# Half of q as a seventeenth pair of seven products, with new places and engines for the last tiles' block sums

## The chip, the cores and the metric

The kernel runs on one core of a Trainium2 chip. The metric is the device time of one execution in microseconds. A core has a matrix engine (TensorE, PE in the profile; PEld is its weight load), three engines for elementwise work (VectorE = DVE, ScalarE = ACT, GpSimd = POOL) and SyncE (SP), which here issues the DMA transfers. Each engine works through its own instructions strictly in order; engines wait for each other by semaphores. Matrix products accumulate in PSUM, which has 8 banks of 128 x 512 float32; GpSimd does not read PSUM in this kernel.

## The reference

One layer of an encoder over a sequence of 1024 positions (a 16 x 64 grid) with 1024 channels, in float32:

```python
h = layer_norm(x, emb_ln_g, emb_ln_b)
proj = h @ w_in                                   # 1024 x 5120
q, k, v, z_a, u, z_b, g_a, g_b = jnp.split(proj, offs, axis=-1)
attn = neighbourhood_attention(q, k, v, rpb)      # 8 heads x 64, window 8 x 16, q scaled by 1/8
y_a = attn * silu(z_a)
u = centred_depthwise_conv(u, conv_w, conv_b)
hr = rg_lru(u, ..., False) + rg_lru(u, ..., True) # gated linear recurrence, both directions
y_b = hr * silu(z_b)
m = sigmoid(g_a + b_merge[0]) * (y_a @ w_ba) + sigmoid(g_b + b_merge[1]) * (y_b @ w_bb)
return layer_norm(ALPHA * h + m @ w_out, ln_g, ln_b)
```

q, k, v, z_a, u and z_b have 512 columns each, g_a and g_b 1024 each. The change concerns the 512 columns of q, which are four blocks (m = 0 to 3) of 128.

## The kernel before

**Precision.** A float32 operand is split into a high part (rounded to fp32r) and a low part (the rest, `lo_of`). A product of two operands is three matrix products, high x high, low x high, high x low (`mm3`).

**Stage 1: normalize, turn, v and half of q.** The sequence is eight tiles of 128 positions. Each tile is normalized, transposed on PE (`turn`, two banks `tp` per tile) and stored transposed as four blocks B11, B12, B21, B22: the first index is the half of the 1024 input channels, the second the half of the sequence. ACT makes the high parts (`turn_hi`), DVE the low parts (`turn_lo`, from the bank). v is computed tile by tile (`v_part`, 24 products), q by blocks of 128 columns and halves of the sequence (`q_part(m, n)`: 8 channel blocks x 3 = 24 products of 128 x 512 in one bank). `q_hi`, `q_lo` and `q_store` scale a q result by 1/8, split it and store it (512 KB).

**Block sums.** For tiles 4 to 7 the second stage needs sums of the four blocks, T1 to T4: `t_full(i)` makes T1, T2, T3 (one ACT copy from PSUM into a place for T3, then four DVE instructions, three of which read PSUM), `t_last(i)` makes T4 (two DVE instructions, both operands in SBUF), `t_hi` casts the high parts on ACT, `t_lo` subtracts the low parts on GpSimd. The T3 copies of all four tiles have the tag "a22" with two places, of which one still holds a weight tile of v until v is done.

**Stage 2: sixteen pairs of seven products.** The other columns are computed two blocks (256 columns) at a time, in the manner of Strassen and Winograd: a pair takes seven products (`OPS`: a11, a12, s2, s1, s3, s4, a22) of 4 channel blocks x 3 = 12 matrix products, where plain multiplication takes eight. Weights of a pair are four loads of 256 KB (`s_load`), four sums (`s_sum`, DVE, operands in SBUF), seven high parts (`s_hi`) and seven low parts (`s_lo`). For pair 0 the high parts are made on ACT, before the loop; for later pairs most are made on GpSimd, one pair ahead. Seven slots of the loop make a pair: in slot k product k runs on PE, the bank of product k - 1 is emptied (`evacuate`: ACT copies u1, u2, u3, DVE additions, then what the pair's `take_...` does with the result), and work for the next pair is issued. Products accumulate into one another's banks (`INTO`: s2, s3 and a22 into the bank of a11, s4 into that of s1), so that a bank has to be read out between two of them.

**Work spread over the slots.** `at(slot, ...)` puts the convolution (`conv_stage`) and the recurrence (`gate_stage`) beside the products; CONV_AT, GATE_AT, LATE_AT and HEAD_AT are their first slots. `U_PAIRS` are the pairs whose result is u; they need no extra bank. The constants of the recurrence (sp, nsp, from `lru_lambda`) are some 30 small DVE instructions issued at once ahead of the loop (lines 626 to 642).

**Order and places.** The order of all engines is the order of the program text. PSUM banks of stage 1 come from the pool ps0 (four banks, assigned by the list `places`) and pst0 (four banks); the loop uses psd (two banks) and ps6 (six banks), which lie over the old ones, and a new tile waits only for the tile whose bank it takes. The tag "x" has five places of 4 KB per partition, used by the input tiles and then by the block sums T1, T2 and T4.

**Around the join** the order is: v of tiles 4 and 5 with `tile_in` of 6 and 7 between, v of 6 and 7 (lines 559 to 592), then `q_part` for (0,1), (1,1), (2,0), (2,1), (3,0), (3,1) with the preparation of pair 0 spread between them (lines 593 to 612), the loads of pair 1, the new pools, the rates, and the loop.

## Time and profile before

| what | us |
|---|---|
| median of 3 runs | 678.4 (678.39 to 678.75) |
| profiled execution, its own time | 678.46 |
| its span, first to last instruction | 676.7 |
| PE busy | 665.2 |
| stage 1 up to the first product of a pair | 0 to 105.4 |
| the sixteen pairs | 105.4 to 426.2 |
| attention, with the first merge products as filling | to 541.9 |
| merge and output projection | to 676.7 |

Times within the execution are counted from the start of the span. A line of a timeline gives start, duration, engine, line of the code, operation, output <- inputs, shapes, and in brackets how long the engine had been idle and what ended that. The chain of waits gives start, duration and what ran. A matrix product of 128 x 512 shows 0.39 us from its start to its end, but the next one starts before that end; the distance of starts is what counts.

### The profile page before, as it was taken

The numbers are of one execution on the slowest core, as the hardware profiler recorded it, in microseconds if no ns is written. First come the engines' busy times: TensorE is split into PE (matmuls) and PEld (weight loads), VectorE is DVE, ScalarE is ACT, GpSimd is POOL, SyncE is SP. The second block draws the span as 40 slices with busy tenths as digits, with TensorE's granted clock in tenths as the row PEclk, the third lists the DMA queues.
The fourth block names the chain that finished last, engine by engine and source line by source line (L and its number), as shares of the span: only waits on it lengthen the run. The fifth ranks groups of instructions, "written<-read, shape, count | busy, mean of one in ns | idle before, by whom it ended". The sixth has DMA issues, their size and how long they took to land.

```text
span 676.7 us, 9344 instructions
## 1 busy us (share of the span) xinstructions
PE 665.2 (98%) x3201; PEld 555.7 (82%) x3201; DVE 492.7 (73%) x821; ACT 364.5 (54%) x612; POOL 355.8 (53%) x258
## 2 busy tenths in 40 slices
PE   8999999999999999999999999999999999999995
PEld 6888888888888887888788888888888878888884
DVE  6978747886998699879967785477787787443434
ACT  6554433256786676669576634477777554210110
POOL 6798632434677576567647444116155456334442
PEclk9999999999999999999999999999999999999998
DMA  8654353233434133431553456998793467412211
GB/s 326 244 179 170 122 206 126 77 110 123 125 128 144 40 103 115 170 126 48 195 178 122 173 191 254 316 366 296 255 323 132 162 220 281 178 62 94 93 63 62
DMA packets 48702, 113.39 MB, mean 168 GB/s; under 512 B 5056, under 2 KB 9744, under 8 KB 47120
## 3 DMA queue, kind: packets, MB, share of 16 engines
q1 hardware_dynamic: 48624, 112.81, 47.2%
q8 instruction: 25, 0.41, 0.3%
q14 instruction: 21, 0.17, 0.1%
q10 hardware_dynamic: 32, 0.01, 0.0%
HBM read 77.11 MB, written 35.68 MB: 167 GB/s over the span
## 4 chain that ended last, share of the span: by engine, by line
PE 89%; DVE 6%; DMA 2%; issue 1%; SPq 1%; ACT 0%; POOL 0%; DVEq 0%; POOLq 0%
PE a L134 30%; PE o L134 13%; PE mb L134 12%; PE s L134 11%; PE q L134 6%; PE v L328 6%; PE acc L1107 3%; PE s L1061 3%; PE pt L1083 3%; PE g L759 2%; DMA wqk_s<-in_w_qk_dram 2%; DVE ws_l L128 1%; PE tp L270 1%; DMA rsb<-rs_d 1%; DVE uc L717 1%
## 5 line engine op out<-in xcount | busy, mean ns | idle before, releaser
L134 PE MATMUL o<-wo_h,ml 128*128 128x512 f32 (+1 forms) x136 | 51.2, 377 | 0.0
L134 PE MATMUL o<-wo_l,mh 128*128 128x512 f32 (+1 forms) x136 | 51.2, 376 | 0.0
L134 PE MATMUL o<-wo_h,mh 128*128 128x512 f32 (+1 forms) x136 | 51.2, 376 | 0.0
L134 PE MATMUL a<-ht_h,ws_h 128*128 128x512 f32 x128 | 50.0, 390 | 0.0
L134 PE MATMUL a<-ht_l,ws_h 128*128 128x512 f32 x128 | 49.8, 389 | 0.0
L134 PE MATMUL a<-ht_h,ws_l 128*128 128x512 f32 x128 | 49.8, 389 | 0.0
L134 PE MATMUL a<-b_h,wa_h 128*128 128x512 f32 x128 | 49.8, 389 | 0.0
L134 PE MATMUL a<-b_h,wa_l 128*128 128x512 f32 x128 | 49.8, 389 | 0.0
L134 PE MATMUL a<-b_l,wa_h 128*128 128x512 f32 x128 | 49.8, 389 | 0.0
L1071 DVE CUSTOM_DVE_ANT_0 sc<-s,bias 128x384 f32<-128x384 f32 (+1 forms) x64 | 33.4, 522 | 21.6 <-PE s L1061 14.2
L1361 DVE SCALAR_TENSOR_TENSOR z<-z,o 128x512 f32<-128x512 f32 (+1 forms) x17 | 11.2, 656 | 51.0 <-PE o L134 51.0
L1091 ACT CAST pt_h<-pt 128x384 fp32r<-128x384 f32 x64 | 29.0, 453 | 25.3 <-PE pt L1083 17.3
L1371 POOL TENSOR_TENSOR z<-z,gb 128x1024 f32<-128x1024 f32 x7 | 16.8, 2400 | 48.5 <-ACT z L1370 48.5
L1076 ACT ACTIVATE p<-sc,summ 128x384 f32<-128x384 f32 (+1 forms) x64 | 37.8, 591 | 5.5 <-DVE summ L1071 5.3
L1340 ACT ACTIVATE sd<-mv,eps_z 128x1 f32<-128x1 f32 x8 | 2.4, 294 | 67.1 <-DVE mv L1366 67.1
L128 DVE TENSOR_TENSOR pt_l<-pt,pt_h 128x384 fp32r<-128x384 f32 x64 | 33.2, 519 | 2.1 <-ACT pt_h L1091 1.6
L328 PE MATMUL v<-wv,b_h 128*128 128x512 f32 x128 | 32.9, 398 | 0.6 <-ACT b_h L279 0.5
L867 POOL CAST wb_h<-wb 128x512 fp32r<-128x512 f32 x9 | 7.0, 779 | 47.4 <-DMA wb<-in_w_bb_dram 47.4
L1061 PE MATMUL s<-ks,qs 128*128 128x384 f32 (+1 forms) x128 | 31.4, 327 | 0.0
L1083 PEld LDWEIGHTS pt<-ident,p 128*128 128x128 f32 x176 | 23.1, 140 | 8.5
L1083 PE MATMUL pt<-ident,p 128*128 128x128 f32 x176 | 29.6, 272 | 0.0
L128 POOL TENSOR_TENSOR wb_l<-wb,wb_h 128x512 fp32r<-128x512 f32 x16 | 22.0, 1375 | 14.3 <-ACT wb_h L865 13.6
(438 smaller groups left out, 2204.2 us busy)
## 6 DMA issues: line engine op xcount, KB each, us to landing
ks<-k_d SPq DMA_DIRECT2D x8, 1024.0 KB, 7.5
h_d<-x SPq DMA_DIRECT2D x8, 512.0 KB, 5.0
v_d<-vs SPq DMA_DIRECT2D x8, 512.0 KB, 3.7
q_d<-q SPq DMA_DIRECT2D x8, 512.0 KB, 3.1
ga_d<-ga SPq DMA_DIRECT2D x16, 256.0 KB, 2.2
gb_d<-gb SPq DMA_DIRECT2D x16, 256.0 KB, 2.6
k_d<-k SPq DMA_DIRECT2D x8, 512.0 KB, 3.4
qs<-q_d SPq DMA_DIRECT2D x8, 512.0 KB, 5.5
```

What stands on the lines that cost most here:

```text
L128: eng.tensor_tensor(lo, full, hi.bitcast(F32), ALU.subtract)
L134: PE.matmul(o, a, b, start=first and i == 0, stop=last and i == len(prods) - 1, skip_group_check=not (first and last))
L328: PE.matmul(vos[i][:], a, wv[kind == "w"][k][:], start=vn[i] == 0, stop=vn[i] == 23)
L759: PE.matmul(o[:, n, :], w[:, 2 * d + b, :], us[b][:, n * HALF:(n + 1) * HALF], start=z == 0, stop=z == 1)
L1061: PE.matmul(o[:, :P * len(near(t))], q[:, t * P:(t + 1) * P], k[:, z, keys], start=z == 0, stop=z == 1)
L1071: V.tensor_tensor_reduce(s[:, :w], o[:, :w], heads[h][2][:, b0:b0 + w], -1.0, 3.0e38, ALU.add, ALU.min, accum_out=sums[h][0][:, t:t + 1])
L1076: A.activation(probs[h % 2][t][:], scs.pop((h, t))[:, :w], AF.Exp, bias=sums[h][0][:, t:t + 1], scale=-1.0, accum_out=sums[h][1][:, t:t + 1])
L1083: PE.transpose(tp[:, n * P:(n + 1) * P], probs[h % 2][t][:, z * P:(z + 1) * P], ident[:])
L1091: A.copy(pt[0][:, span(b)], tps[h, b][:, :P * len(near(b))])
L1107: PE.matmul(acc[g][:, d:d + w], vvs[h // 2][:, b, h % 2, :], pt[:, a:a + w], start=b in (1, 6) and z == 0, stop=z == 1 and b == (4, 7)[g])
L1361: V.scalar_tensor_tensor(z[:, cols], z[:, cols], ALPHA * TWICE, o, ALU.mult, ALU.add)
L1371: G.tensor_tensor(z[:], z[:], gb2[:, 0, :], ALU.mult)
```

## The change

The number of pairs becomes 17. Pair 0 is now the q columns of blocks m = 2 and 3 (a new `take_q`), which `q_part` computed before; all other pairs move up by one, and with them the slots of the convolution, the recurrence and what follows (by seven). `qk_load(2)`, `qk_load(3)` and their `qk_prep` go.

Around it: the four weight blocks of pair 0 are loaded into two "x" places instead of their usual ones; its sums stand ahead of v of tile 7, its high and low parts between v of tile 7 and the two q groups that are left, (0,1) and (1,1); all its low parts are made on DVE. The T3 copies of tiles 4 to 7 get the tags a22, a21, a12, a22. `t_last` of tiles 5, 6 and 7 goes from DVE to GpSimd and moves, with `t_hi`, `t_lo` and `t_full`, to other places in the order. The rates become a generator whose six parts are issued in slots 1 to 6.

```diff
-N_PAIR = 16
+N_PAIR = 17
-CONV_AT = (7, 24, 45, 66)
-GATE_AT = (14, 24, 35, 45, 56, 66, 77, 87)
-LATE_AT = (102, 102, 103, 104, 105)
-HEAD_AT = 109
+CONV_AT = (14, 31, 52, 73)
+GATE_AT = (21, 31, 42, 52, 63, 73, 84, 94)
+LATE_AT = (109, 109, 110, 111, 112)
+HEAD_AT = 116
-U_PAIRS = (0, 5)
+U_PAIRS = (1, 6)
...
     def t_full(i):
-        tt[i, 3] = wsp.tile([P, 4, P], F32, tag="a22", bufs=2, name=f"t3_{i}")[:]
+        tag = ("a22", "a21", "a12", "a22")[i - 4]
+        tt[i, 3] = wsp.tile([P, 4, P], F32, tag=tag, bufs=2 if tag == "a22" else 1, name=f"t3_{i}")[:]
...
     def t_last(i):
-        t4 = tt[i, 4]
-        V.tensor_tensor(t4, f(B21[0], i), tt[i, 2], ALU.subtract)
-        V.tensor_tensor(t4, t4, f(B21[1], i), ALU.add)
+        t4, eng = tt[i, 4], V if i == 4 else G
+        eng.tensor_tensor(t4, f(B21[0], i), tt[i, 2], ALU.subtract)
+        eng.tensor_tensor(t4, t4, f(B21[1], i), ALU.add)
...
     def s_load(p, *names):
+        for z, o in enumerate(names if p < N_PAIR else ()):
+            if p:
+                t = wsp.tile([P, 4, P], F32, tag=o, bufs=2 if o == "a22" else 1, name=f"{o}_{p}f")[:]
+            else:
+                if z == 0:
+                    both = ln.tile([P, 2, 4, P], F32, tag="x", bufs=5, name=f"{o}_{p}f")
+                t = both[:, z]
+            SP.dma_start(t, w_s[p, ("a11", "a21", "a12", "a22").index(o)])
...
     def s_lo(p, o):
         if p < N_PAIR:
             hi, lo = s_w[p, o]
-            lo_of(G if o in LO_POOL else V, lo[:], s_a[p, o][:], hi[:])
+            lo_of(G if p and o in LO_POOL else V, lo[:], s_a[p, o], hi[:])
```

The order from `q_store(0, 0)` to the loop, after the change (before, `t_last(5)` follows `q_store(1, 0)`, and the other steps stand as described above):

```python
    keep(7)
    t_full(5)
    q_part(1, 0)
    t_last(5)
    q_hi(1, 0); q_lo(1, 0); q_store(1, 0)
    for kind in "hwa": v_part(4, kind, KS)
    tile_in(6)
    v_hi(4)
    t_hi(5, 2, 1, 3)
    tile_lo(6)
    v_lo(4); v_store(4)
    t_full(6)
    t_hi(5, 4)
    t_lo(5, 2, 1, 3, 4)
    t_last(6)
    for kind in "hwa": v_part(5, kind, KS)
    tile_in(7)
    v_hi(5)
    t_hi(6, 2, 1, 3)
    tile_lo(7)
    v_lo(5); v_store(5)
    t_full(7)
    t_hi(6, 4)
    t_lo(6, 2, 1, 3, 4)
    t_last(7)
    s_load(0, "a21", "a22"); s_load(0, "a11", "a12"); s_load(1, "a21")
    for kind in "hwa": v_part(6, kind, KS)
    v_hi(6); v_lo(6); v_store(6)
    t_hi(7, 2, 1, 3)
    s_sum(0, "s1", "s2", "s3", "s4")
    for kind in "hwa": v_part(7, kind, KS)
    s_load(1, "a12")
    v_hi(7); v_lo(7); v_store(7)
    for o in OPS[:3]: s_hi(0, o); s_lo(0, o)
    t_hi(7, 4)
    t_lo(7, 2, 1, 3, 4)
    s_load(1, "a11"); s_load(1, "a22")
    q_part(0, 1)
    for o in OPS[3:5]: s_hi(0, o); s_lo(0, o)
    q_hi(0, 1); q_lo(0, 1); q_store(0, 1)
    q_part(1, 1)
    for o in OPS[5:]: s_hi(0, o); s_lo(0, o)
    q_hi(1, 1); q_lo(1, 1); q_store(1, 1)
```

And in the loop:

```diff
+    def take_q():
+        def consume(mi, n, add, o, c=None):
+            c = o if c is None else c
+            if add is not None:
+                V.tensor_tensor(c[:], add[:], o[:], ALU.add)
+            t = lru.tile([P, 2, HALF], F32R, tag=("us0", "r", "i", "us1")[2 * mi + n], name=f"q2{mi}{n}")
+            def high():
+                A.activation(t[:, 0, :], c[:], AF.Copy, scale=0.125)
+            def store():
+                V.scalar_tensor_tensor(t[:, 1, :], c[:], 0.125, t[:, 0, :].bitcast(F32), ALU.mult, ALU.subtract)
+                SP.dma_start(q_d[2 + mi][:, :, halves[n]], t[:].bitcast(F32))
+            return [high, store]
+        return consume
...
-    takes = [lambda: take_u(0), lambda: take_zg(zb_d, 0, "zb"), ...
+    takes = [take_q, lambda: take_u(0), lambda: take_zg(zb_d, 0, "zb"), ...
+    rates = decay_rates()
+    for slot in range(1, 7):
+        at(slot, 1, lambda: next(rates))
...
-    heads = [16, 20, 12, 24, 26, 18, 32, 22, 28, 34, 4, 30, 6, 14, 36, 38]
+    heads = [2, 16, 20, 12, 24, 26, 18, 32, 22, 28, 34, 4, 30, 6, 14, 36, 38]
```

More of the change, by code (lines that the diff above doesn't have):

```diff
@@ L369, in s_load @@
     def s_load(p, *names):
-        for o in names if p < N_PAIR else ():
-            t = wsp.tile([P, 4, P], F32, tag=o, bufs=2 if o == "a22" else 1, name=f"{o}_{p}f")
-            SP.dma_start(t[:], w_s[p, ("a11", "a21", "a12", "a22").index(o)])
+        for z, o in enumerate(names if p < N_PAIR else ()):
[6 more added lines that the diff above has]
+            SP.dma_start(t, w_s[p, ("a11", "a21", "a12", "a22").index(o)])
             s_a[p, o] = t
@@ L378, in s_sum @@
                             s3=("a11", "a21", ALU.subtract), s4=("a12", "s2", ALU.subtract))[o]
-            t = s_a[p, o] = wsp.tile([P, 4, P], F32, tag=o, name=f"{o}_{p}f")
-            V.tensor_tensor(t[:], s_a[p, a][:], s_a[p, b][:], op)
+            t = s_a[p, o] = wsp.tile([P, 4, P], F32, tag=o, name=f"{o}_{p}f")[:]
+            V.tensor_tensor(t, s_a[p, a], s_a[p, b], op)
     def s_hi(p, o):
@@ L384, in s_hi @@
             s_w[p, o] = pair(wsp, [P, 4, P], f"w{o}_{p}", tag="w" + o)
-            (G.tensor_copy if p and o in HI_POOL else A.copy)(s_w[p, o][0][:], s_a[p, o][:])
+            (G.tensor_copy if p and o in HI_POOL else A.copy)(s_w[p, o][0][:], s_a[p, o])
     def s_lo(p, o):
@@ L532, in encoder_kernel @@
     keep(5)
-    qk_load(2)
     tile_in(4)
@@ L552, in encoder_kernel @@
     keep(7)
+    t_full(5)
     q_part(1, 0)
-    t_full(5)
+    t_last(5)
     q_hi(1, 0)
@@ L557, in encoder_kernel @@
     q_store(1, 0)
-    t_last(5)
     for kind in "hwa":
@@ L562, in encoder_kernel @@
     v_hi(4)
-    t_hi(5, 2, 1, 3, 4)
-    t_lo(5, 2, 1, 3, 4)
+    t_hi(5, 2, 1, 3)
     tile_lo(6)
@@ L568, in encoder_kernel @@
     t_full(6)
+    t_hi(5, 4)
+    t_lo(5, 2, 1, 3, 4)
+    t_last(6)
     for kind in "hwa":
@@ L573, in encoder_kernel @@
     t_hi(6, 2, 1, 3)
-    t_lo(6, 2, 1, 3)
     tile_lo(7)
@@ L577, in encoder_kernel @@
     v_store(5)
-    t_last(6)
+    t_full(7)
     t_hi(6, 4)
-    t_lo(6, 4)
-    t_full(7)
+    t_lo(6, 2, 1, 3, 4)
+    t_last(7)
+    s_load(0, "a21", "a22")
+    s_load(0, "a11", "a12")
+    s_load(1, "a21")
     for kind in "hwa":
@@ L584, in encoder_kernel @@
     v_hi(6)
-    t_last(7)
     v_lo(6)
     v_store(6)
+    t_hi(7, 2, 1, 3)
+    s_sum(0, "s1", "s2", "s3", "s4")
     for kind in "hwa":
         v_part(7, kind, KS)
+    s_load(1, "a12")
     v_hi(7)
@@ L592, in encoder_kernel @@
     v_store(7)
-    s_load(0, "a11")
-    for m in range(4):
-        for n in BOTH if m > 1 else (1,):
-            q_part(m, n)
-            if m < 2:
-                qk_prep(m + 2)
-                if m == 0:
-                    qk_load(3)
-                    t_hi(7, 2, 1, 3, 4)
-                    t_lo(7, 2, 1, 3, 4)
-                    s_load(0, "a21", "a22", "a12")
-                else:
-                    s_sum(0, "s1", "s2", "s3", "s4")
-            q_hi(m, n)
-            q_lo(m, n)
-            q_store(m, n)
-            if m > 1:
-                for w in (OPS[:2], OPS[2:4], OPS[4:6], OPS[6:])[2 * (m - 2) + n]:
-                    s_hi(0, w)
-                    s_lo(0, w)
-    s_load(1, "a11", "a21", "a12", "a22")
+    for o in OPS[:3]:
+        s_hi(0, o)
+        s_lo(0, o)
+    t_hi(7, 4)
+    t_lo(7, 2, 1, 3, 4)
+    s_load(1, "a11")
+    s_load(1, "a22")
+    q_part(0, 1)
+    for o in OPS[3:5]:
+        s_hi(0, o)
+        s_lo(0, o)
+    q_hi(0, 1)
+    q_lo(0, 1)
+    q_store(0, 1)
+    q_part(1, 1)
+    for o in OPS[5:]:
+        s_hi(0, o)
+        s_lo(0, o)
+    q_hi(1, 1)
+    q_lo(1, 1)
+    q_store(1, 1)
     for pl in (ln, wpl, hb12, pst, ps0):
@@ L625, in encoder_kernel, with decay_rates @@
     lam = sm[:, SM_LAM:SM_LAM + 8]
-    V.tensor_scalar(smh[:], sm[:], 0.5, None, ALU.mult)
-    V.tensor_scalar(t0[:], lam, -1.0, None, ALU.mult)
-    V.tensor_tensor(t0[:], lam, t0[:], ALU.min)
-    A.activation(t0[:], t0[:], AF.Exp)
-    V.tensor_scalar(t1[:], t0[:], 2.0, None, ALU.add)
-    V.reciprocal(t1[:], t1[:])
-    V.tensor_tensor(t0[:], t0[:], t1[:], ALU.mult)
-    V.tensor_tensor(t1[:], t0[:], t0[:], ALU.mult)
-    V.tensor_scalar(t2[:], t1[:], 1.0 / 21.0, 1.0 / 19.0, ALU.mult, ALU.add)
-    for n in (17, 15, 13, 11, 9, 7, 5, 3, 1):
-        V.tensor_tensor(t2[:], t2[:], t1[:], ALU.mult)
-        V.tensor_scalar(t2[:], t2[:], 1.0 / n, None, ALU.add)
-    V.tensor_tensor(t2[:], t2[:], t0[:], ALU.mult)
-    V.tensor_scalar(t0[:], lam, -1.0, 0.0, ALU.mult, ALU.max)
-    V.scalar_tensor_tensor(t0[:], t2[:], 2.0, t0[:], ALU.mult, ALU.add)
-    V.tensor_scalar(sp[:], t0[:], C_LRU, None, ALU.mult)
-    V.tensor_scalar(nsp[:], t0[:], -C_LRU, None, ALU.mult)
+    def decay_rates():
+        V.tensor_scalar(smh[:], sm[:], 0.5, None, ALU.mult)
+        V.tensor_scalar(t0[:], lam, -1.0, None, ALU.mult)
+        V.tensor_tensor(t0[:], lam, t0[:], ALU.min)
+        A.activation(t0[:], t0[:], AF.Exp)
+        yield
+        V.tensor_scalar(t1[:], t0[:], 2.0, None, ALU.add)
+        V.reciprocal(t1[:], t1[:])
+        V.tensor_tensor(t0[:], t0[:], t1[:], ALU.mult)
+        V.tensor_tensor(t1[:], t0[:], t0[:], ALU.mult)
+        V.tensor_scalar(t2[:], t1[:], 1.0 / 21.0, 1.0 / 19.0, ALU.mult, ALU.add)
+        yield
+        for n in (17, 15, 13, 11, 9, 7, 5, 3, 1):
+            V.tensor_tensor(t2[:], t2[:], t1[:], ALU.mult)
+            V.tensor_scalar(t2[:], t2[:], 1.0 / n, None, ALU.add)
+            if n in (13, 7, 1):
+                yield
+        V.tensor_tensor(t2[:], t2[:], t0[:], ALU.mult)
+        V.tensor_scalar(t0[:], lam, -1.0, 0.0, ALU.mult, ALU.max)
+        V.scalar_tensor_tensor(t0[:], t2[:], 2.0, t0[:], ALU.mult, ALU.add)
+        V.tensor_scalar(sp[:], t0[:], C_LRU, None, ALU.mult)
+        V.tensor_scalar(nsp[:], t0[:], -C_LRU, None, ALU.mult)
+        yield
     ups, ucs, hsum = {}, {}, {}
@@ L902, in gates_b @@
         return lambda: take_zg(gb_d, 2 * j, "gb", SM_BM + 8)
-    takes = [lambda: take_u(0), lambda: take_zg(zb_d, 0, "zb"), lambda: take_zg(za_d, 0, "za"), gates_a(0), gates_a(1),
+    takes = [take_q, lambda: take_u(0), lambda: take_zg(zb_d, 0, "zb"), lambda: take_zg(za_d, 0, "za"), gates_a(0), gates_a(1),
              lambda: take_u(2), gates_b(0), lambda: take_zg(zb_d, 2, "zb"), gates_a(2), gates_b(1),
              lambda: take_k(0), gates_a(3), lambda: take_k(2), lambda: take_zg(za_d, 2, "za"), gates_b(2), gates_b(3)]
+    rates = decay_rates()
+    for slot in range(1, 7):
+        at(slot, 1, lambda: next(rates))
     for t, slot in enumerate(CONV_AT):
```

## The prediction

> **What bounds the kernel now.** I read the page's first two parts, then the chain of waits in order of time, then what PE waited for, then the timelines of PE, GpSimd (POOL), VectorE (DVE) and ScalarE (ACT) around the stretch that is rebuilt.

> ```profile
> span 676.7 us, 9344 instructions
> PE 665.2 (98%) x3201; PEld 555.7 (82%) x3201; DVE 492.7 (73%) x821; ACT 364.5 (54%) x612; POOL 355.8 (53%) x258
> PE   8999999999999999999999999999999999999995
> ```

> PE is busy from end to end. The chain says the same of the stretch in question:

> ```profile
> 62.03 10.90 PE v L328 x48
> 72.93 32.64 PE q L134 x144
> 105.57 8.16 PE a L134 x36
> 113.73 2.72 PE s L134 x12
> ...
> 119.17 2.72 PE s L134 x12
> 121.89 10.88 PE a L134 x48
> ```

> The six remaining q groups (144 products) and the first pair of seven products follow without a gap. One wait of PE in the pair loop is listed at all, and the longest anywhere is 1.0 us:

> ```profile
> PE clock L202 <- DVE zero L160: 1.0, 1, 1.0
> PE a L134 <- DVE w L792: 0.4, 1, 0.4
> ```

> So a product less is time less, and a new wait of PE is time more: nothing else moves the end. The starts of the first q product, the 49th, and the first product of the pairs give the pace:

> ```profile
> 72.77 0.39 PE L134 MATMUL q<-b_h,wqk_h 128*128 128x512 f32 x1
> ...
> 83.64 0.39 PE L134 MATMUL q<-b_h,wqk_h 128*128 128x512 f32 x1
> ...
> 105.41 0.39 PE L134 MATMUL a<-b_h,wa_h 128*128 128x512 f32 x1
> ```

> (105.41 - 72.77) / 144 = 0.2267 us per product.

> **What is removed.** The channel blocks m = 2 and 3 of q cost 2 x 2 x 24 = 96 products in q_part; as a pair they cost 7 x 12 = 84. Twelve products less are 12 x 0.2267 = 2.72 us. This is the only gain on PE's path. Also gone: two qk_load of 512 KB, two qk_prep (one ACT and one POOL instruction each); they lay beside PE.

> **What is only moved, at no cost.** Everything indexed by pair shifts by one pair and by seven slots (CONV_AT, GATE_AT, LATE_AT, HEAD_AT, U_PAIRS), so each later slot has the work it had. The four q results lose q_hi, q_lo and q_store ahead of the loop and get take_q inside it: per result an ACT cast, a DVE low part and a 512 KB store, and on DVE three additions more. The stores stand ahead of the loads of pair 2 and 3 in SP's queue, which have 8 us until they are used (three slots of 2.72), against this landing time:

> ```profile
> q_d<-q SPq DMA_DIRECT2D x8, 512.0 KB, 3.1
> ...
> a_0f<-in_w_s_dram SPq DMA_DIRECT2D x4, 256.0 KB, 5.3
> ```

> **The rates.** In the kernel before they are one run on DVE from 106.84 to 115.6, and the addition that has to empty the a11 bank before the seventh product (start 105.41 + 6 x 2.72 = 121.73) ended at 121.47:

> ```profile
> 106.84 1.28 DVE L626 TENSOR_SCALAR smh<-sm 128x60 f32<-128x60 f32 x1
> ...
> 109.73 0.17 DVE L636 TENSOR_TENSOR sp<-sp,sp 128x8 f32<-128x8 f32 x1
> 109.93 0.17 DVE L637 TENSOR_SCALAR sp<-sp 128x8 f32<-128x8 f32 x1
> ...
> 115.42 0.17 DVE L642 TENSOR_SCALAR nsp<-sp 128x8 f32<-128x8 f32 x1
> ...
> 120.79 0.68 DVE L658 TENSOR_TENSOR up<-u,a 128x512 f32<-128x512 f32 x1
> ```

> One follows the other by 0.20 us. Spread over slots 1 to 6 they put some 1 to 2 us into each slot of 2.72. In slot 4 stand 0.7 (low part), 0.7 (take_q's) and six rates at 0.20, so that the addition of slot 5 starts on time with some 2 us to spare. I cost this at nothing; with the cover gone it would be what DVE is late, 0 to 1 us.

> **Own places of the t3 copies.** ACT's copy for tile 5 waited for POOL to be done with tile 4's:

> ```profile
> 49.62 1.66 ACT L314 CAST ht_h<-t 128x512 fp32r<-128x512 f32 x3 [1.34 <-DVE t L304]
> ...
> 57.21 0.59 ACT L301 COPY t<-tp 128x512 f32<-128x512 f32 x1 [3.03 <-POOL ht_l L128]
> ```

> It starts 3 us sooner. PE waited for none of it, so the gain is 0, but t_last, t_lo and what follows start sooner too, which I use below.

> **Late block sums on POOL: the dear part.** A DVE instruction with two operands in SBUF takes 0.69 us while POOL is idle (58.55, 66.77) and 1.45 to 1.78 us while POOL computes (61.08, 62.56, 312.13):

> ```profile
> 52.93 5.50 POOL L128 TENSOR_TENSOR ht_l<-t,ht_h 128x512 fp32r<-128x512 f32 x4
> 60.70 5.94 POOL L128 TENSOR_TENSOR ht_l<-t,ht_h 128x512 fp32r<-128x512 f32 x4 [2.27 <-ACT ht_h L314]
> ...
> 81.91 5.02 POOL L128 TENSOR_TENSOR ht_l<-t,ht_h 128x512 fp32r<-128x512 f32 x4
> ```

> ```profile
> 58.55 0.69 DVE L303 TENSOR_TENSOR t<-t,b_l 128x512 f32<-128x512 f32 x1
> ...
> 61.08 1.45 DVE L309 TENSOR_TENSOR t<-b_h,t 128x512 f32<-128x512 f32 x1
> 62.56 1.67 DVE L310 TENSOR_TENSOR t<-t,b_l 128x512 f32<-128x512 f32 x1
> ...
> 66.77 0.69 DVE L303 TENSOR_TENSOR t<-t,b_l 128x512 f32<-128x512 f32 x1
> ```

> ```profile
> 311.62 1.74 POOL L128 TENSOR_TENSOR wa_l<-a_10f,wa_h 128x512 fp32r<-128x512 f32 x1
> ...
> 312.13 1.78 DVE L380 TENSOR_TENSOR s_11f<-a_11f 128x512 f32<-128x512 f32 x1
> ```

> Four POOL instructions take 5.02 us alone (1.255 each) and 5.94 with two such DVE instructions among them, so each DVE instruction costs POOL (5.94 - 5.02) / 2 = 0.46. They take turns: POOL 1.25, DVE 0.45, so while both have work each gets one instruction per 1.70 us. The DVE rows that read PSUM (0.67 to 0.69 under the same POOL rows) are not held.

> [...]

> POOL's row now runs without a pause. It starts t_lo of tile 4 at 52.93 as before: 5.50 + 0.46 (one DVE turn of tile 5) ends at 58.9; t_last of tile 5, 2 x 1.255, at 61.4; t_lo of tile 5, 5.02 + 0.46, at 66.9; t_last of tile 6, 2.51 + 0.46, at 69.9. ACT waits there in t_hi(6, 4), and behind that in its queue stands v_hi(6): two casts of 0.55 (three take 1.66) give 71.0, and v_lo(6) on DVE (0.69) 71.7. POOL still has nine instructions (three of tile 6, t_last and four t_lo of tile 7), the last ending near 86.

> Behind v_lo(6) DVE now has the sums and low parts of pair 0, which before were spread from 89.28 to 102.7, where the first met a POOL instruction (1.85) and the rest took 0.69:

> ```profile
> 89.28 1.85 DVE L380 TENSOR_TENSOR s_0f<-a_0f 128x512 f32<-128x512 f32 x1 [5.33 <-DMA a_0f<-in_w_s_dram]
> 91.17 0.69 DVE L380 TENSOR_TENSOR s_0f<-s_0f,a_0f 128x512 f32<-128x512 f32 x1
> ...
> 101.40 1.28 DVE L128 TENSOR_TENSOR ws_l<-s_0f,ws_h 128x512 fp32r<-128x512 f32 x2
> ```

> They are four s_sum and, up to q_lo(0,1), five s_lo (a11, a12, s2, s1, s3), nine instructions with two SBUF operands. The first gets its turn at about 72.3, the ninth 8 x 1.70 later, at 85.9, and ends at 86.5; q_lo(0,1) ends at 87.2. The casts they need are ready: t_last of tile 7 ends at 79.1, t_hi(7, 4) behind it at 79.7. The loads of pair 0 are issued once t_lo(5) has freed their places (64 to 67) and land by 72.4 at 5.3 us, just in time.

> **Who waits for q_lo(0,1).** It empties the bank of q(0,1). The first product of the pairs needs a bank of the new pool of six, which lies over the old ones. In the kernel before it started with no gap at 105.41 while the last q bank was still being read until 106.92, but the last but one had been empty since 101.49:

> ```profile
> 100.80 0.69 DVE L360 SCALAR_TENSOR_TENSOR q<-q,q 128x512 fp32r<-128x512 f32 x1 [1.41 <-ACT q L355]
> ...
> 106.23 0.69 DVE L360 SCALAR_TENSOR_TENSOR q<-q,q 128x512 fp32r<-128x512 f32 x1 [3.55 <-ACT q L355]
> ```

> By the addresses in the compiled kernel before (no row of the profile) it takes the last but one, the third of the four of ps0. After the change the same turn in `places` gives that bank to q(0,1). So product a11 of pair 0, which could start at 83.64, starts at about 87.2: a new wait of 3.5 us. Bounds: 0 if the bank is another; 4.5 if the loads land 1 us later than 5.3. I take 3.5, since the bank follows from the same code. The operands of the later products are in time: a12's low part at 81, T2's of tile 7 near 81 against a start at 92.6, T4's at 86 against 103.5.

> **Sum.** The profiled execution took 678.46 us (span 676.7 and 1.8 around it), 0.06 above the median of the three runs, 678.4. 678.46 - 2.72 + 3.5 = 679.2; I say 679.3 with the small gaps of a first pair. Its own range is 678.3 to 680.2 (a wait of 2.6 to 4.5).

> **Rivals.**
> No wait at the join: a11 takes another bank, or DVE gets more turns than I count. For it: the old join had no gap. Against it: the nine turns. 678.46 - 2.72 = 675.7; a wait under 1.3 us stays below 677.04.

> The loads of pair 0 land late: 512 KB of v_store are ahead of them, and rows of 256 KB took 5.3. From 72.3 on every us later moves all nine turns; 1.3 us later gives 680.6. Against it, the DMA engines were busy 4 and 3 tenths in slices 4 and 5 (51 to 85 us):

> ```profile
> DMA  8654353233434133431553456998793467412211
> ```

> PE's clock drops in the gap (the slower side). PE stands still from 83.81 to 87.2, 3.4 us, where the longest wait was 1.0. At the start of the kernel the trace shows PE at half pace, sixteen products in 3.20 us against 1.91 for the same shape later:

> ```profile
> 4.29 3.20 PE L211 MATMUL gps<-ident,gb_col 128*128 128x128 f32 x16
> ...
> 26.32 1.91 PE L270 MATMUL tp<-ident,x 128*128 128x128 f32 x16
> ```

> If the pause brings that back for the 3 to 6 us that it lasted there, half of it is lost: 1.5 to 3 more, 680.8 to 682.3, I say 681.4. It decides once the gap is long enough; no row here shows how long. [...]

> **Chances.** Forecast 0.48; no wait or one under 1.3 us 0.27; late loads 0.10; clock 0.12; others 0.03. A measurement of this kernel can tell about 0.2% (1.36 us) from no change: 677.04 to 679.76. The forecast's own range lies within it for some three quarters, above it for the rest. Faster: 0.27 and some of the others, 0.28. Slower: 0.13 + 0.10 + 0.12 = 0.35. Within: 0.37. The range takes in the first rival's 675.7 and most of the clock's: 675.5 to 681.6.

> **What would show it.** Right: a PE gap of some 3.5 us ahead of the first a<-b_h,wa_h product, released by DVE L360 (q_lo); DVE's L380 and L128 rows between 72 and 87 at 1.6 to 1.8 us, POOL's at 1.7; 84 products where 96 were. The forecast is wrong if that product starts by 84.5, if it is released by something else, or if the products after it are spaced over 0.23 us. A time under 677 would say that DVE was early or that the bank is another.

## The result, and the profile after

The changed kernel takes 681.56 us, median of six runs (680.93 to 683.36); the kernel before, on the same chip, 678.42 (678.05 to 679.0). The ratio is 1.0049 with a 95% interval of 1.0036 to 1.0062: slower by some 3.3 us. The profiled execution took 681.59 us, with a span of 679.8.

Busy times and the slices of PE and of its granted clock (the share of the full clock that PE was given), from the page of the changed kernel:

```profile
PE 665.5 (98%) x3189; PEld 555.8 (82%) x3189; DVE 503.9 (74%) x829; ACT 365.0 (54%) x615; POOL 362.7 (53%) x267
PE   8999989999999999999999999999999999999995
PEclk9999979999999999999999999999999999999998
```

The twelve products are gone (3189 instructions of PE for 3201), yet PE's busy time has not fallen (665.5 for 665.2). Two digits say where to look: slice 6 (85 to 102 us) has an 8 for PE and a 7 for its granted clock. In the kernel before both are 9 there; its clock:

```profile
PEclk9999999999999999999999999999999999999998
```

The list of PE's waits in the same run has one new row, at its top:

```profile
PE a L134 <- DVE q L361: 3.3, 1, 3.3
```

That is the wait that the prediction named: the first product of the pairs behind q_lo. VectorE's and GpSimd's timelines show how it comes about:

```profile
71.58 1.28 DVE L386 TENSOR_TENSOR s_0f<-a_0f 128x512 f32<-128x512 f32 x1
72.89 1.67 DVE L386 TENSOR_TENSOR s_0f<-s_0f,a_0f 128x512 f32<-128x512 f32 x1
74.48 1.78 DVE L386 TENSOR_TENSOR s_0f<-a_0f 128x512 f32<-128x512 f32 x1
76.17 1.78 DVE L386 TENSOR_TENSOR s_0f<-a_0f,s_0f 128x512 f32<-128x512 f32 x1
77.87 0.68 DVE L128 TENSOR_TENSOR vs<-v,vs 128x512 fp32r<-128x512 f32 x1
78.47 2.88 DVE L128 TENSOR_TENSOR wa_l<-a_0f,wa_h 128x512 fp32r<-128x512 f32 x2
81.28 5.14 DVE L128 TENSOR_TENSOR ws_l<-s_0f,ws_h 128x512 fp32r<-128x512 f32 x3
86.34 0.68 DVE L361 SCALAR_TENSOR_TENSOR q<-q,q 128x512 fp32r<-128x512 f32 x1
```

```profile
77.48 1.62 POOL L311 TENSOR_TENSOR t<-t,b_l 128x512 f32<-128x512 f32 x1
79.06 6.81 POOL L128 TENSOR_TENSOR ht_l<-t,ht_h 128x512 fp32r<-128x512 f32 x4
```

Four sums and five low parts, each with two operands in SBUF, take turns with GpSimd; three of them in one row take 5.14 us, 1.71 each, and GpSimd's four take 6.81, 1.70 each. The low part vs, which reads PSUM, takes 0.68 in the midst of it. GpSimd's row ends at 85.87, and the next two low parts of DVE behind that (86.95 and 87.55) take 0.68 each; in e3 below, with six instructions fewer on GpSimd, the three take 0.63 each. q_lo(0,1) starts at 86.34.

What comes behind the wait stands in PE's timeline:

```profile
83.35 0.39 PE L134 MATMUL q<-b_l,wqk_h 128*128 128x512 f32 x1
87.08 0.80 PE L134 MATMUL a<-b_h,wa_h 128*128 128x512 f32 x1 [3.34 <-DVE q L361]
87.67 0.63 PE L134 MATMUL a<-b_h,wa_l 128*128 128x512 f32 x1
88.10 0.63 PE L134 MATMUL a<-b_l,wa_h 128*128 128x512 f32 x1
...
92.36 0.47 PE L134 MATMUL a<-b_h,wa_h 128*128 128x512 f32 x1
92.68 0.39 PE L134 MATMUL a<-b_h,wa_l 128*128 128x512 f32 x1
```

After the last q product the next could have been issued at 83.35 + 0.23 = 83.58; it was issued at 87.08, 3.50 later. From 87.08 to 92.68 thirteen products are issued in 5.60 us; at 0.2267 they would take 2.95, so 2.65 us are lost to half pace. The account: 678.46 - 2.72 + 3.50 + 2.65 = 681.9, against 681.59.

The same stretch in windows of 3.41 us, half of the time that the clock is half here (columns: the window and its length, busy us and count of PE, PEld, DVE, ACT, POOL, then the granted clock, DMA share and GB/s), cut where the clock changes:

```profile
82.29:85.70 3.41, 1.45 (x7) 0.87 (x5) 3.41 (x3) 0.63 (x2) 3.41 (x3) 1.00 0.15 58
85.70:89.11 3.41, 2.03 (x5) 1.66 (x6) 3.41 (x6) 0.00 (x0) 0.17 (x1) 0.50 0.26 98
89.11:92.52 3.41, 3.41 (x10) 2.67 (x9) 1.35 (x5) 0.00 (x0) 0.00 (x0) 0.50 0.56 210
92.52:95.93 3.41, 3.41 (x17) 2.79 (x16) 0.46 (x1) 2.60 (x4) 0.50 (x1) 1.00 0.02 5
```

The clock falls to half at 85.70, two microseconds into the pause, while PE still stands still, and comes back at 92.52. It is half for 6.82 us. The profile shows one of the six runs. Its mean granted clock is 0.992. Of the others, three have 0.992 or 0.993; no run of a kernel without a pause, here or below, is under 0.995. The last two have 0.995, which does not tell them apart.

### The profile page after: what moved, and what is told of

Same layout as the page of the kernel before. It is cut to its first block, busy times and chain, and to the rows that moved or that the text cites. A ratio compares the mean times of both kernels' runs of the same rounds, so it can differ in the third digit from the quotient of the medians.

```text
span 679.8 us, 9357 instructions
## 1 busy us (share of the span) xinstructions
PE 665.5 (98%) x3189; PEld 555.8 (82%) x3189; DVE 503.9 (74%) x829; ACT 365.0 (54%) x615; POOL 362.7 (53%) x267
## 4 chain that ended last, share of the span: by engine, by line
PE 89%; DVE 7%; issue 2%; DMA 1%; SPq 1%; ACT 0%; DVEq 0%
PE a L134 32%; PE o L134 13%; PE mb L134 13%; PE s L134 12%; PE v L329 5%; PE acc L1145 4%; PE s L1099 3%; PE pt L1121 3%; PE g L794 2%; PE q L134 2%; DMA wqk_s<-in_w_qk_dram 1%; DVE ws_l L128 1%; DVE wa_l L128 1%; PE tp L270 1%; DVE uc L752 1%
## 5 line engine op out<-in xcount | busy, mean ns | idle before, releaser
L134 PE MATMUL a<-b_h,wa_h 128*128 128x512 f32 x136 | 54.2, 398 | 3.3 <-DVE q L361 3.3
L134 PE MATMUL a<-b_h,wa_l 128*128 128x512 f32 x136 | 53.9, 397 | 0.0
L134 PE MATMUL a<-b_l,wa_h 128*128 128x512 f32 x136 | 53.9, 396 | 0.0
L134 PE MATMUL a<-ht_h,ws_h 128*128 128x512 f32 x136 | 53.1, 390 | 0.0
L134 PE MATMUL a<-ht_h,ws_l 128*128 128x512 f32 x136 | 53.0, 390 | 0.0
L134 PE MATMUL a<-ht_l,ws_h 128*128 128x512 f32 x136 | 52.9, 389 | 0.0
L134 PE MATMUL o<-wo_h,ml 128*128 128x512 f32 (+1 forms) x136 | 51.2, 377 | 0.0
L134 PE MATMUL o<-wo_l,mh 128*128 128x512 f32 (+1 forms) x136 | 51.2, 377 | 0.0
L134 PE MATMUL o<-wo_h,mh 128*128 128x512 f32 (+1 forms) x136 | 51.2, 377 | 0.0
L128 DVE TENSOR_TENSOR pt_l<-pt,pt_h 128x384 fp32r<-128x384 f32 x64 | 33.2, 519 | 2.1 <-ACT pt_h L1129 1.6
L134 PEld LDWEIGHTS a<-b_h,wa_h 128*128 128x128 f32 x136 | 26.2, 193 | 9.4 <-DVE q L361 3.8
L134 PEld LDWEIGHTS a<-b_h,wa_l 128*128 128x128 f32 x136 | 26.2, 193 | 5.5
L134 PEld LDWEIGHTS a<-b_l,wa_h 128*128 128x128 f32 x136 | 26.1, 192 | 5.5
## 6 DMA issues: line engine op xcount, KB each, us to landing
h_d<-x SPq DMA_DIRECT2D x8, 512.0 KB, 4.9
v_d<-vs SPq DMA_DIRECT2D x8, 512.0 KB, 3.2
q_d<-q SPq DMA_DIRECT2D x8, 512.0 KB, 3.6
ga_d<-ga SPq DMA_DIRECT2D x16, 256.0 KB, 2.2
gb_d<-gb SPq DMA_DIRECT2D x16, 256.0 KB, 2.4
k_d<-k SPq DMA_DIRECT2D x8, 512.0 KB, 3.4
qs<-q_d SPq DMA_DIRECT2D x8, 512.0 KB, 5.4
```

The source lines that it names most:

```text
L128: eng.tensor_tensor(lo, full, hi.bitcast(F32), ALU.subtract)
L134: PE.matmul(o, a, b, start=first and i == 0, stop=last and i == len(prods) - 1, skip_group_check=not (first and last))
```

## The experiments

All are edits of the changed kernel. Ratios are to the kernel before on the same chip; pause and half pace are those of the profiled run, in which the pause is the idle time ahead of a11 and half pace counts products about 0.43 us apart.

| run | edit | ratio (95%) | pause, us | at half pace |
|---|---|---|---|---|
| the change | none | 1.0049 (1.0036 to 1.0062) | 3.3 | 12 |
| e1 | q_lo(0,1) earlier | 0.9964 (0.9951 to 0.9977) | 0 | 0 |
| e5 | another bank for q(0,1) | 0.9969 (0.9958 to 0.9980) | 0 | 0 |
| e9 | e1 and e5 | 0.9958 (0.9941 to 0.9974) | 0 | 0 |
| e2 | pause filled with 14 products | 1.0019 (1.0009 to 1.0028) | 0 | 0 |
| e11 | 6 products in the pause | 1.0040 (1.0027 to 1.0053) | 1.9 | 0 |
| e6 | 3 products in the pause | 1.0039 (1.0026 to 1.0052) | 2.7 | 7 |
| e12 | q_lo(0,1) later | 1.0066 (1.0051 to 1.0081) | 4.6 | 10 |
| e3 | sums back on VectorE | 0.9989 (0.9979 to 0.9999) | 1.6 | 0 |
| e4 | q_lo(0,1) a little earlier | 0.9999 (0.9989 to 1.0008) | 1.6 | 0 |
| e10 | e1, sums back on VectorE | 0.9961 (0.9946 to 0.9976) | 0.3 | 0 |
| e8 | e1, old places | 1.0054 (1.0039 to 1.0070) | 3.4 | 13 |
| e7 | e1, rates at once | 1.0017 (1.0007 to 1.0026) | 0 | 0 |

### Where the wait comes from: order and bank (e1, e5, e9)

e1 puts q_hi, q_lo and q_store of q(0,1) ahead of three of the low parts:

```diff
-    for o in OPS[:3]: s_hi(0, o); s_lo(0, o)
+    for o in OPS[:2]: s_hi(0, o); s_lo(0, o)
...
     q_part(0, 1)
-    for o in OPS[3:5]: s_hi(0, o); s_lo(0, o)
     q_hi(0, 1); q_lo(0, 1); q_store(0, 1)
+    for o in OPS[2:5]: s_hi(0, o); s_lo(0, o)
     q_part(1, 1)
```

> Theory: the first product waits only because q_lo(0,1) stands behind the low parts of pair 0 on DVE. Here q_hi, q_lo and q_store of (0,1) stand ahead of the low parts of s2, s1 and s3. q_lo(0,1) should then end near 82, before the last q product starts at 83.4; no wait at the first product, no products at half pace, 678.4 - 2.7 = 675.7 (up to 676.2). Rival: something else of the join is late as well (the low part of a12, T2's or T1's of tile 7), and the wait comes back at the second, third or fourth product: 677 to 681.

VectorE in e1: q_lo at 82.50, and the three low parts with s4's behind it:

```profile
82.50 0.68 DVE L361 SCALAR_TENSOR_TENSOR q<-q,q 128x512 fp32r<-128x512 f32 x1
83.10 5.19 DVE L128 TENSOR_TENSOR ws_l<-s_0f,ws_h 128x512 fp32r<-128x512 f32 x4
```

There is no wait of PE at the join, and the ratio is 0.9964. e1 leaves the bank as it is and moves only the order on DVE and ACT (and q's store). e5 does the reverse: it changes the list of banks alone, so that q(0,1) uses the first bank of ps0, and the third is left by v of tile 4.

```diff
-    places = itertools.chain((0, 1, 2, 3, 0, 1, 2, 0, 2, 3, 1), itertools.cycle((2, 3, 0, 1)))
+    places = iter((0, 1, 2, 3, 0, 1, 2, 0, 2, 3, 1, 2, 3, 0, 1, 0, 3))
```

> The changed kernel with another turn of banks for the last six q groups: q(0,1) now uses the first bank of the four of ps0, and the third, which a11 of pair 0 takes over, is left by v of tile 4 long before. DVE's order and POOL's work stay as in the changed kernel, so that q_lo(0,1) should still be late, near 87. Theory (the wait is a11's for that one bank): PE runs on without a pause at 83.6, no half pace behind it, and the time is 678.5 - 2.7 = 675.8 on the scale of the kernel before. Rival (the first products need something else that DVE brings late, such as a low part, or a later product of pair 0 takes q(0,1)'s new bank): the wait moves by a product group or two and stays above 1.5 us, 678 to 681.6.

q_lo(0,1) of e5 on VectorE, and then the join on PE:

```profile
86.94 0.68 DVE L361 SCALAR_TENSOR_TENSOR q<-q,q 128x512 fp32r<-128x512 f32 x1
```

```profile
83.97 0.39 PE L134 MATMUL q<-b_l,wqk_h 128*128 128x512 f32 x1
84.19 0.39 PE L134 MATMUL a<-b_h,wa_h 128*128 128x512 f32 x1
```

q_lo is as late as in the changed kernel, and a11 follows q's last product 0.22 us later. So a11 waited for nothing else of DVE's than the emptied bank.

> The changed kernel with both remedies: q_lo(0,1) ahead of the low parts of s2, s1 and s3, and q(0,1) in a bank that a11 does not take. If both remove the same pause (theory), the time is that of either alone, 0.9965 of the kernel before, 676.5. If they work in different ways (rival), it goes below 0.994.

With both, the ratio is 0.9958, within the intervals of either alone: two ways to remove one pause, and no second gain that these runs can tell.

### What the pause costs beside its length (e2, e6, e11, e12)

e2 fills the pause with fourteen products whose result is not read (e6 with 3, e11 with 6 of them); DVE's work stays.

```diff
+    idle = ps0.tile([P, HALF], F32, tag="b0", bufs=1, name="idle")
+    for _ in range(14):
+        PE.matmul(idle[:], qk_w[1][0][:, 0, :], B11[0][:, 0, :], start=True, stop=True)
     for pl in (ln, wpl, hb12, pst, ps0):
```

> Fourteen products that nobody reads (128x512, into a bank that is free) fill most of the 3.4 us in which PE stood still; the order on the other engines is that of the changed kernel. Theory: the first product of the pairs still starts at about 87.1, released by q_lo(0,1), but the twelve products behind it are spaced by 0.227 us instead of 0.427, since PE did not stand still: 681.6 - 2.4 = 679.2. Rival: the half pace has another cause than the pause (the new bank, the other operands): it stays, 681.6.

PE's timeline of e2:

```profile
84.03 3.33 PE L627 MATMUL idle<-b_h,wqk_h 128*128 128x512 f32 x14
87.51 0.50 PE L134 MATMUL a<-b_h,wa_h 128*128 128x512 f32 x1
87.84 0.39 PE L134 MATMUL a<-b_h,wa_l 128*128 128x512 f32 x1
```

a11 still waits for q_lo and starts at 87.51 (87.08 in the changed kernel), but the next product follows 0.33 us later, not 0.59, those after that are 0.23 us apart, and the ratio falls from 1.0049 to 1.0019, by 2.0 us. With PE busy in the pause the pace holds, at the same operands and banks, so the half pace of the changed kernel goes with PE's idleness there and not with those.

> The changed kernel with three products whose result nobody reads at the end of q's last group, so that PE's pause ahead of a11 is about 0.7 us shorter: some 2.7 us where it was 3.3, with the same DVE and POOL work and the same start of a11 near 87.1. Theory A (half pace comes only once a pause is as long as 3.3 us): the products behind it are 0.23 us apart, and the time is 2.4 us below the changed kernel's, 679.2. Theory B (half pace comes from a pause of about half that already, as single runs with a pause of 1.6 us hint): a dozen products 0.43 us apart as in the changed kernel, 681.6. In between, some runs each way, if where the pause falls on a clock of its own decides.

e6's pause is 2.65 us, and half pace comes all the same. The cuts in its windows are again where the clock changes:

```profile
84.15:87.56 3.41, 1.00 (x5) 0.50 (x3) 3.41 (x3) 0.60 (x1) 2.45 (x2) 1.00 0.00 0
87.56:90.98 3.42, 3.18 (x8) 2.50 (x9) 3.39 (x8) 0.00 (x0) 0.00 (x0) 0.50 0.47 177
90.98:94.39 3.41, 3.41 (x16) 2.81 (x15) 0.24 (x2) 2.04 (x3) 0.00 (x0) 1.00 0.35 130
```

Theory A (only a pause as long as 3.3 brings it) falls: the ratio is that of the change. But half pace lasts 3.42 us here, just half of the 6.82 before.

> The changed kernel with q_hi, q_lo and q_store of q(0,1) behind all low parts of pair 0. Two more DVE instructions of 0.68 us stand ahead of q_lo, so that PE's pause grows from 3.3 to about 4.6 us. Theory A (the half pace behind the pause lasts longer with the length of the pause, 7 products after 2.7 us and 12 after 3.3): over 16 products at 0.43 us, 683.5 to 684.5. Theory B (it lasts for a window that does not depend on the pause): 7 to 14 products, so 682 to 683.3.

e12 moves q_hi, q_lo and q_store(0,1) behind the last low parts (OPS[5:]). The pause is 4.6 us. Its windows:

```profile
82.55:85.96 3.41, 1.14 (x6) 0.60 (x4) 3.41 (x3) 0.60 (x1) 3.34 (x2) 1.00 0.05 18
85.96:89.37 3.41, 1.08 (x3) 0.89 (x4) 3.41 (x6) 0.00 (x0) 0.00 (x0) 0.50 0.00 0
89.37:92.78 3.41, 3.41 (x10) 2.64 (x9) 1.11 (x5) 0.00 (x0) 0.00 (x0) 0.50 0.83 308
92.78:96.19 3.41, 3.41 (x17) 2.81 (x16) 0.00 (x0) 2.60 (x4) 0.01 (x1) 1.00 0.03 5
```

Half clock lasts 6.82 us again, from 85.96 to 92.78, though the pause is 1.3 us longer than in the changed kernel; PE only stands still for more of it, so that ten products fall into it and not twelve. The time, 683.41 us, lies between the two ranges given, 0.1 from either; the ten products decide it for theory B, since A asked for over sixteen. The stretches of half clock are 3.42 or 6.82 us, one or two times 3.41, whatever the pause. Each begins where the 3.41 us before it held 1.45, 1.00 or 1.14 us of PE's work (the change, e6, e12). The last section has the distance from the clock's return to its next fall.

> The changed kernel with six products whose result nobody reads at the end of q's last group: a pause of PE of about 2.0 us, between 1.6 (no half pace in the two profiles that have it) and 2.7 (seven products at half pace). Theory A (the half pace begins at some length of the pause, and lasts longer the longer the pause): 0 to 5 products 0.43 us apart; the unread products and the rest of the pause still cost 3.3, so 679 to 680.5. Theory B (a fixed window somewhere between, on a clock of its own): single runs differ by about 2 us from one another, 679 in some and 681.5 in others.

e11's profiled run has a pause of 1.95 us and no product at half pace. Its ten runs spread more than those of any other kernel here: three took 679.52 to 679.88, seven 681.10 to 683.29, while the kernel before lay between 677.81 and 679.39 beside them. 678.46 - 2.72 + 3.5 = 679.2 is what the three come near to; the seven have some 2 us or more on top. That speaks for theory B, by which at this length it hangs on where the pause falls. The profile shows one of the three alone, and its clock is 1.00 throughout from 83 to 97. Of the seven, five have a mean granted clock of 0.993 to 0.995, where the kernel before has 0.996 to 0.998 in all its runs beside them: these five bear out the half pace. The other two (681.10 and 682.46) have 0.996 and 0.997 and show no sign of it; why they are slow stays open.

### What GpSimd's sums bring (e3, e4, e10)

```diff
-        t4, eng = tt[i, 4], V if i == 4 else G
+        t4, eng = tt[i, 4], V
```

> t_last of all four tiles on DVE again, all else as changed. Theory: what is late is DVE's queue ahead of q_lo(0,1); six instructions more on DVE and six fewer on POOL leave q_lo(0,1) at 85.5 to 87, so a wait of 2 to 3.3 us stays; 677.7 to 681.5. Rival: the block sums on POOL are the cause by themselves: q_lo(0,1) ends before 83.6, no wait, 675.7.

e3, with the order of the change, has q_lo at 84.98 and a pause of 1.65 us, under the 2 to 3.3 expected. DVE starts its sums of pair 0 five microseconds later there (76.67 for 71.58), but GpSimd has six instructions fewer, and the three low parts take 1.88 us, 0.63 each, for 5.14 in the changed kernel:

```profile
83.18 1.88 DVE L128 TENSOR_TENSOR ws_l<-s_0f,ws_h 128x512 fp32r<-128x512 f32 x3
```

e4 gets the same pause by moving q_lo(0,1) behind s1's low part:

> q_lo(0,1) one turn earlier: ahead of the low part of s3, behind that of s1. Theory: the first product starts one turn of 1.7 us earlier, at 85.4, after a wait of 1.7; that pause is half as long and PE keeps its pace: 675.7 + 1.7 = 677.4. Rival: any pause over 1 us halves the pace for some us: 677.4 + 2.4 = 679.8.

PE at the join of e3, then of e4:

```profile
85.72 0.50 PE L134 MATMUL a<-b_h,wa_h 128*128 128x512 f32 x1 [1.65 <-DVE q L361]
86.05 0.39 PE L134 MATMUL a<-b_h,wa_l 128*128 128x512 f32 x1
```

```profile
85.83 0.50 PE L134 MATMUL a<-b_h,wa_h 128*128 128x512 f32 x1 [1.61 <-DVE q L361]
```

Neither has half pace in its profile; in each, one run of ten is some 2 us above the median (679.87 and 680.33), and it has the lowest granted clock of the ten, 0.994 and 0.995 for 0.996 to 0.998. In both, a11 is issued 1.8 us late, and -2.72 + 1.8 would make the ratio 0.9986. e3's 0.9989 agrees; e4's 0.9999 is 0.9 us above it, and what takes that time is not shown. Either way e4's rival, half pace after any pause over 1 us, falls with the profile.

> The kernel with q_lo(0,1) ahead of the low parts of s2, s1 and s3 (no pause of PE), and in it the last block sums t_last back on DVE. Theory: the move to GpSimd matters by the pause alone, so that without a pause the time stays at 0.9965 of the kernel before, 676.5. Rival (DVE, with six more instructions ahead of the copies and casts of the last tiles, is then late for something of tile 7 or of pair 0): a wait of PE of 1 us or more, 677.5 or over.

e10 joins e1's order with the sums on VectorE: 0.9961, as e1's 0.9964. The move to GpSimd brings nothing measurable where there is no pause; in the change's own order it made q_lo 1.4 us later (86.34 for 84.98) and so brought the pause from 1.65 us, with no half pace in the profile, to 3.34, with twelve products of it.

### The own places (e8)

```diff
-        tag = ("a22", "a21", "a12", "a22")[i - 4]
+        tag = "a22"
```

> The kernel with q_lo(0,1) ahead of the low parts of s2, s1 and s3 (no pause of PE), and in it the four t3 copies back in the two places that they had before. The forecast put the own places at nothing for PE, since PE waited for none of these copies. By that the time stays at 0.996 of the kernel before, 676. The rival: with the block sums on POOL the copy of tile 6 would wait until POOL is done with tile 4, and so on for tile 7, which moves t_last of tile 7 and the casts behind it by some 4 us, q_lo(0,1) from 82.5 to 86 to 88, and brings PE's pause back: 3 to 4.5 us, and half pace for a dozen products if it is over 3 us: 679 to 682.

With e1's order and t3's old places the ratio is 1.0054 where e1's is 0.9964: 6 us. ACT's copies of t3 wait for GpSimd, and with the sums on it the second one shown (tile 6) gets its place only at 66.55:

```profile
57.20 0.59 ACT L302 COPY t<-tp 128x512 f32<-128x512 f32 x1 [3.02 <-POOL ht_l L128]
...
66.55 0.59 ACT L302 COPY t<-tp 128x512 f32<-128x512 f32 x1 [4.89 <-POOL ht_l L128]
```

e1 makes that copy at 61.72. All behind it is late, q_lo(0,1) starts at 87.51 (e1: 82.50), and PE pauses for 3.4 us and runs at half pace for thirteen products:

```profile
88.25 0.79 PE L134 MATMUL a<-b_h,wa_h 128*128 128x512 f32 x1 [3.44 <-DVE q L361]
...
93.53 0.63 PE L134 MATMUL a<-b_h,wa_h 128*128 128x512 f32 x1
93.96 0.45 PE L134 MATMUL a<-b_h,wa_l 128*128 128x512 f32 x1
```

Old places with the sums on VectorE were not tried.

### The rates (e7)

e7 is e1 with `for _ in decay_rates(): pass` ahead of the loop in place of one part in each of six slots.

> The kernel with q_lo(0,1) ahead of the low parts of s2, s1 and s3 (no pause of PE), and in it the decay rates made at once ahead of the loop, as in the kernel before, in place of six slots. The forecast's step says that the spread is worth nothing as long as DVE has room, and 0 to 1 us if it hasn't. Some 43 small DVE instructions at 0.2 us are 8.7 us in one run, from about 89 to 98; the addition that frees the first a bank is due at 83.6 + 6 x 2.72 = 100. If DVE then has the low part, take_q's two and the addition behind it (about 3 us), PE waits 0 to 1.2 us: 676 to 678 on the scale of the kernel before. The rival (the casts that stand behind the rates delay the second pair's high or low parts too): 678 to 680, with a wait of PE past the first pair.

The ratio is 1.0017 against e1's 0.9964, 3.6 us more and above what the expectation gave to the forecast's step. (The run has 31 DVE instructions, not the 43 of the expectation; its 8.8 us include 1.60 of waiting for ACT.) PE's waits in e7:

```profile
PE a L134 <- ACT u L976: 1.7, 1, 1.7
...
PE s L134 <- ACT u L982: 0.8, 1, 0.8
...
PE a L134 <- DVE c L704: 0.4, 1, 0.4
```

Most of it goes through ACT, whose timeline shows why:

```profile
88.57 1.28 ACT L642 ACT_TABLE_LOAD   x1 [4.43 <-DVE sp L641]
89.86 0.21 ACT L642 ACTIVATE sp<-sp 128x8 f32<-128x8 f32 x1
89.98 0.57 ACT L976 COPY u<-a 128x512 f32<-128x512 f32 x1
```

The exponential of the rates has a load of ACT's table ahead of it (1.28 us) and stands in ACT's queue ahead of the copy that empties the first bank. It waits for three small DVE instructions that stand behind q_lo(1,1), and the copy with it. In slot 1, where the change puts it, it stands behind that copy. The second wait is ACT's too (u behind a cast that waits for DVE's addition, which stands behind the rates until 98.06).

## Why the prediction came out wrong

**The product count and the chain to the wait were right.** Twelve products at 0.2267 us, 2.72: with no pause (e10: 0.3 us) e1, e5, e9 and e10 stand at 0.9958 to 0.9969, 2.1 to 2.9 us less. The loads were in time, the turns with GpSimd came at 1.70 (eight from 72.86 to 86.42), and a11 took q(0,1)'s bank: the nine instructions were to end at 86.5 and ended at 86.42, q_lo at 87.2 and ended at 87.02, and a11, to start at about 87.2, started at 87.08. The low part of v's last tile (vs, 0.68 us), which the prediction left out, fell between two turns and cost none. e5 shows the bank, which the prediction had from no row of the profile, e1 the order. The added pause was 3.50 us for the 3.5 taken.

**What failed is the step on PE's clock.** The sum, 678.46 - 2.72 + 3.5, has no term for it; half pace stands only as the third rival with a chance of 0.12, and no row of before showed how long a pause has to be for it. It took 2.65 us. That PE's clock would drop in the gap, and the price, were right: 1.5 to 3 us more, 681.4 in all, against 2.65 and 681.56. It came in the profiled run, and none of the six runs is as fast as the forecast (680.93 is the fastest). The time lies inside the stated 675.5 to 681.6 only because that range took in most of this rival. What the kernel before could not show, the runs after it do: in the four profiles with half pace (the change, e6, e8, e12) the 3.41 us before the fall held 0.99 to 1.45 us of PE's work (e8's 0.99 by the same cut), 29 to 43% of it, and the clock was half for 3.42 or some 6.82 us. In the last section 1.45 us of work is the most that is followed by a fall, and 1.56 the least that is not. With a limit of 1.5 us and windows of 3.41 a pause of 3.34 us leaves too little work in one window at some six of seven places where it can fall (an estimate from these figures), and the rival would have been the forecast. Without the half clock the forecast stands: e2, with the same late a11, is 1.0019, which on 678.42 is 679.7 for the 679.3 predicted.

**"The gain is 0" for the own places** holds for PE's waits of before, where the prediction read it, and it used the earlier starts that the places allow in its sum. As the price of the part it is wrong: with the sums on GpSimd and e1's order the places are worth 6 us (e8).

**"0 to 1 us" for the rates with their cover gone** was short by far: 3.6 us (e7). The bound counted what DVE would be late and not the ACT instruction among them, nor what is queued behind that on ACT. The zero for the change as it stands held, since the spread avoids it.

**The rival without a wait** (0.27, 675.7) is what e1 and e5 are, by one small edit each; the one with late loads did not occur: pair 0's blocks landed 3.5 us after their issue (median) for the 5.3 taken, and the first sum waited for none of them.

## What to carry to other kernels

Price a pause of the matrix engine at its length and at the half pace that can follow it: here, behind a stretch of 3.41 us with 1.45 us of work or less, another 1.4 to 2.6 us (7 to 13 products at 0.2 us more in the change, e6, e8 and e12); cutting 3.3 us to 1.6 was worth more than the 1.7 (4.1 in e3 and 3.4 in e4, by the ratios). Where a pool of banks takes over another's places, look which result was the last in the bank that the first product takes, and put its evacuation early or give it another bank: either was worth over 5 us here. Work that is moved to an idle engine is not free: here the low parts on VectorE, with two operands in SBUF, took 1.71 us each beside GpSimd's and 0.68 behind its last, and the move made nothing measurably faster and lengthened the pause from 1.65 to 3.34 us.

## What was not expected of the hardware

**PE's work ahead of a fall.** The clock falls while PE still stands still, 2.0 us after its last product in the changed kernel (83.74 to 85.70), and the window before that held 1.45 us of work. The end of a kernel shows more, since PE's last products fill a part of one window there. In e1, then in e5:

```profile
665.39:668.80 3.41, 1.56 (x14) 1.36 (x12) 1.71 (x7) 0.29 (x1) 0.00 (x0) 1.00 0.38 154
668.80:672.21 3.41, 0.00 (x0) 0.00 (x0) 3.08 (x10) 0.00 (x0) 0.00 (x0) 1.00 0.16 53
```

```profile
665.41:668.82 3.41, 1.40 (x12) 1.20 (x10) 1.87 (x7) 0.29 (x1) 0.00 (x0) 1.00 0.39 154
668.82:672.23 3.41, 0.00 (x0) 0.00 (x0) 2.92 (x9) 0.00 (x0) 0.00 (x0) 0.50 0.21 68
```

Behind 1.56 us of work the clock stays for one more window, behind 1.40 it falls. The end of the changed kernel has 2.26 us in such a window, that of the kernel before 3.03, and the clock stays in both for one more window, which is empty, and then falls. So of these windows at full clock those with 1.45 us of work or less (the change, e5, e6, e8, e12) are followed by half clock, and those with 1.56 or more by full clock. By these figures, with a limit of 1.5, a pause of 1.95 us halves the clock at a little under half of the places where it can fall (an estimate); in e11 the granted clock shows it in five of ten runs.

**What stays open.** The clock stays half through windows with 1.08, 2.03 or 2.38 us of work (e12, the change, e8), and comes back behind one with 3.18 of 3.41 (e6); where between 2.38 and 3.18 it returns, these runs don't settle. A pause of 1.6 us leaves some 1.8 us of work or more in a window, which is over the 1.56 above, yet one run each of e3 and e4 is slow at a lower clock; how long the pause was in those two is not recorded.
